# Attention groups 1 and 2 on tokens sorted by residue modulo 4, and the first large transfers requested by SyncE in order

## The chip, the cores and the metric

The kernel runs on one core of one Trainium2 chip. Its engines are TensorE (PE in the rows; PEld is its weight load), VectorE (DVE), ScalarE (ACT), GpSimd (POOL) and SyncE (SP), which here only requests DMA transfers. The metric is the device time of one launch in microseconds, lower being better. Times of a kernel are medians of several launches. The profile is one further launch, and its own time stands beside the others below.

## The reference, cut to what matters

The program is a model of two layers over 256 tokens of width 2048. Each layer normalises x, multiplies it by a wide matrix `w_in`, feeds four mixers (branches A to D) and merges them:

```python
h = _rmsnorm(x, norm_g); proj = h @ w_in            # 2048 x 17544
ya = _branch_dilated(a_q, a_k, a_v, ...) * silu(a_z)  # A: three groups of 4 heads
yb = _branch_mla(...) * silu(b_z); yc = _branch_mlstm(...) * silu(c_z); yd = _branch_s5(...) * silu(d_z)
up = einsum('bsnw,nwd->bsnd', stack([ya, yb, yc, yd]), w_up)
merged = sum(sigmoid(gate + merge_b) * up, over the branches)
return x + merged @ w_out
```

The change is in branch A. Its three groups have windows and dilations `A_GROUPS = ((128, 1), (512, 4), (2048, 16))`: a query of group 1 sees only keys that are a multiple of 4 tokens back, one of group 2 only those a multiple of 16 back. So in both groups a query sees only keys whose token number has the same residue modulo 4. Each head's scores are `q k / sqrt(128) - slope * distance`, masked, and the groups are joined by their log-sum-exp:

```python
o = einsum(p, v) / den;  lse = m + log(den)         # for each group
w = softmax(stack(lses), axis=0);  out = sum(w[..., None] * o_all, axis=0)
```

Inputs, weights and outputs are float32.

## The kernel before

**Weights.** All weights stream through the core. They are cut into units of 128 x 1024 numbers (512 KB; smaller ones for narrow blocks). SP requests a unit into one of four `raw` buffers; ACT rounds it to `wh` and DVE forms the remainder `wl` (four buffers each, `Stream.split`). PE multiplies each unit in three passes: `wh,hH`, `wl,hH` and `wh,hL`, where `hH` and `hL` are the two parts of the normalised, transposed x. A full unit is 12 such matmuls of 128 x 512. `Stream.get(i)` casts three units ahead of PE and requests six ahead. A column block of `w_in` is eight units, and its result lies in two of the four PSUM banks named `mm`.

**Order of the work.** The program is written out by Python code that keeps a plan of the engines' clocks (`Plan`). The weight matmuls are the backbone. After each unit `tick` lets the branches' generators ("chains" a to d, e for evacuations, m, q) emit a step when the plan says that its inputs are ready. Each engine then runs its instructions in the order written, and each waits only by semaphores. A block that needs a branch's result (`until`) forces the chain on.

**Branch A** (`a_evac`, `a_transposes`, `a_group`, `softmax_pv`). For each group the blocks `aq`, `ak`, `av` give queries, keys and values. q and k are transposed on PE (`tt`) and copied by ACT to `aqT` and `akT`. With 256 tokens there are two query tiles of 128. For each of 4 heads the first tile is multiplied with 128 keys, the second with 256 (`sc`). DVE adds the distance term (`as0`, `as1`), ACT takes the exponential, PE transposes three 128 x 128 pieces per head (`pt`), and three matmuls per head multiply them with the values (`pv`). Group 0 is kept in `aO`; the results of groups 1 and 2 are folded in by `rows`. After group 2 `aO` is divided, gated and transposed for the up projection (`y_split`, `yt`).

**The start.** SP requests the parameters `pp`, then parts of the transposed input `xt` and the first units in turn. ACT scales `xt` to `hH` (`prep_first`). ACT also requests the natural input `xb`, four transfers of 512 KB, and the constants `cc` (`first_squares`); the mean square of x is taken from `xb`, and `r`, its inverse root, is first needed when the evacuations of the first block begin. The framework gives each transfer one of eight semaphores in turn, and a request waits until the transfer eight before it has landed.

The instruction wrapper (`call`, line 258) and the `load` helper (line 277) record nearly everything, so the rows go by tile names.

Of the kernel before, what the change touches and what calls it, by code (L numbers as in the profile page):

```python
# [107 lines left out]
for _nm, _n in (("norm_g", 16), ("aqn", 1), ("akn", 1), ("cqg", 4), ("ckvg", 1), ("bqn", 1), ("bkn", 1),  # L108
                ("bqr", 64), ("bkr", 64), ("convw", 16), ("convb", 4), ("ib", 4), ("fb", 4),
                ("lr", 16), ("li", 16), ("ld", 16), ("dskip", 4)):  # L110
    PP[_nm] = (_o, _o + _n)
    _o += _n
# [4 lines left out]
for _nm, _n in (("dist", 768), ("mb", 256), ("mc", 128), ("iota", 256), ("inv", 32)):  # L117
    CC[_nm] = (_o, _o + _n)
    _o += _n
# [144 lines left out]
def hybrid_kernel(ctx: ExitStack, tc: tile.TileContext, x_in, xt_in, pos, win, wup, wout, wuq, wukv, wglu, pp_in, db_in,  # L264
# [22 lines left out]

    cc = const.tile([P, NCC], F32, tag="cc", name="cc")
    ident = const.tile([P, P], F32, tag="ident", name="ident")
    load(nc.scalar, ident, in_=id_in)  # L290
# [69 lines left out]
    class Stream:  # L360
        DL, SL = 6, 3

        def __init__(self):
            self.raw, self.spl, self.names, self.nd, self.ns = {}, {}, {}, 0, 0

        def dma(self, upto, part=None):
            while self.nd <= min(upto, len(units) - 1):
# [9 lines left out]
                self.nd += 1  # L377

# [76 lines left out]
    def block(key, lhs, K, n):  # L455
# [8 lines left out]
        while k < K:  # L464
            assert units[cur[0]][0] == key, (units[cur[0]][0], key)
            lhs(k, 0)
            if cur[0] and not key[0]:
                lhs(min(k + 4, K - 1), 0)
# [85 lines left out]
    def rotary_tables():  # L554
        V.tensor_tensor(sel, ident[:, 0:4], ident[:, 32:36], op=ALU.add)
        G.memset(Mz.bitcast(F32), 0.0)
        pf = const.tile([P, 2], F32, tag="posf", name="posf")
# [37 lines left out]
    def new_layer(l):  # L595
        o = L()
        o.l, o.after = l, []
        o.pp = parp.tile([P, NPP], F32, tag="pp", name="pp")
        load(nc.scalar if l else nc.sync, o.pp, in_=pp_in[l])
        o.p = lambda nm: o.pp[:, PP[nm][0]:PP[nm][1]]  # L600
# [4 lines left out]
        o.r, o.gL, o.yT = None, None, {}  # L605
        return o

    def load_d(o):
        o.db = s4([P, 2, 16, 16], name="db")
        load(nc.sync if o.l else nc.scalar, o.db, in_=db_in[o.l].rearrange("p (r t c) -> p r t c", r=2, t=16))  # L610
        o.dc = s4([P, 2, 16, 32], name="dc")
        load(nc.sync if o.l else nc.scalar, o.dc, in_=dc_in[o.l].rearrange("p (r t c) -> p r t c", r=2, t=16))
# [100 lines left out]
    def to_T(src, dst, scale=None, nh=4):  # L713

        for t in range(2):
            ps = brps("tt").rearrange("p (k s) -> p k s", s=P)
            for k in range(nh):
                T.transpose(ps[:, k], src[:, t, k * P:(k + 1) * P], ident)
            if scale is None:
                A.copy(dst[:, :, t * P:(t + 1) * P], ps[:, :nh])  # L720
            else:
                A.activation(dst[:, :, t * P:(t + 1) * P], ps[:, :nh], AF.Copy, scale=scale)

    def softmax_pv(s0, s1, v, rows):
# [15 lines left out]
        pT = [h2([P, 4, P], name="pT") for _ in range(3)]  # L740
        for i in range(3):
            ps = brps("pt").rearrange("p (k s) -> p k s", s=P)
            for h in range(4):
                src = s0[:, h] if i == 0 else s1[:, h, (i - 1) * P:i * P]
# [3 lines left out]
        for t in range(2):  # L748
            ps = brps("pv").rearrange("p (k s) -> p k s", s=P)
            for h in range(4):  # L750
                for kt in range(t + 1):
                    T.matmul(ps[:, h], lhsT=pT[t + kt][:, h], rhs=v[:, kt, h * P:(h + 1) * P],
                             start=(kt == 0), stop=(kt == t))
# [4 lines left out]
    def a_evac(o, ps, gain_scale, key):  # L758
# [20 lines left out]
        spawn("a", a_transposes(o, dst, key, scale))  # L779

    def a_transposes(o, src, key, scale):
        yield (src,)
        dst = s4([P, 4, S], name=key)
        to_T(src, dst, scale)
        setattr(o, key, dst)

    def a_group(o, g, v):
        qT, kT = o.aqT, o.akT
        yield (qT, kT)
        dist = c_("dist")[:, g * 256:(g + 1) * 256]  # L790
        s0 = h2([P, 4, P], name="as0")
        s1 = s4([P, 4, S], name="as1")
        ps = brps("sc").rearrange("p (k s) -> p k s", s=P)
        for h in range(4):
            T.matmul(ps[:, h], lhsT=qT[:, h, 0:P], rhs=kT[:, h, 0:P], start=True, stop=True)
        for h in range(4):
            V.scalar_tensor_tensor(s0[:, h], dist[:, P:], -SLOPES[4 * g + h], ps[:, h], op0=ALU.mult, op1=ALU.add)
        for h2_ in range(2):
            ps = brps("sc").rearrange("p (k s) -> p k s", s=S)
            for j in range(2):  # L800
                h = 2 * h2_ + j
                T.matmul(ps[:, j], lhsT=qT[:, h, P:], rhs=kT[:, h, :], start=True, stop=True)
            for j in range(2):
                h = 2 * h2_ + j
                V.scalar_tensor_tensor(s1[:, h], dist, -SLOPES[4 * g + h], ps[:, j], op0=ALU.mult, op1=ALU.add)
        yield
        if g == 0:
            o.aO = s4([P, 2, 4, P], name="aO")
            o.amx = parp.tile([P, 2, 4], F32, tag="amx", name="amx")
            o.aden = parp.tile([P, 2, 4], F32, tag="aden", name="aden")  # L810

        def rows(t, ps, mx, den):
            O = o.aO[:, t]
            if g == 0:
                A.copy(O, ps)
                V.tensor_copy(o.amx[:, t], mx[:, t])
                V.tensor_copy(o.aden[:, t], den[:, t])
                return
            al, be, mn = sm([P, 4], name="al"), sm([P, 4], name="be"), sm([P, 4], name="mn")
            V.tensor_tensor(mn, o.amx[:, t], mx[:, t], op=ALU.max)  # L820
            V.tensor_tensor(al, o.amx[:, t], mn, op=ALU.subtract)
            V.tensor_tensor(be, mx[:, t], mn, op=ALU.subtract)
            A.activation(al, al, AF.Exp)
            A.activation(be, be, AF.Exp)
            V.tensor_copy(o.amx[:, t], mn)
            dn = sm([P, 4], name="dn")
            V.tensor_tensor(dn, den[:, t], be, op=ALU.mult)
            V.tensor_tensor(o.aden[:, t], o.aden[:, t], al, op=ALU.mult)
            V.tensor_tensor(o.aden[:, t], o.aden[:, t], dn, op=ALU.add)
            tmp = h2([P, 4, P], name="atmp")  # L830
            for h in range(4):
                A.activation(tmp[:, h], ps[:, h], AF.Copy, scale=be[:, h:h + 1])
                V.scalar_tensor_tensor(O[:, h], O[:, h], al[:, h:h + 1], tmp[:, h], op0=ALU.mult, op1=ALU.add)

        yield from softmax_pv(s0, s1, v, rows)
# [342 lines left out]
    def d_tables(o):  # L1178
# [4 lines left out]
        load_d(o)  # L1183
        yield (o.pp,)
# [215 lines left out]
    xpool = ctx.enter_context(tc.tile_pool(name="xd", bufs=1, space=bass.MemoryType.DRAM))  # L1400
    x_cur = [x_in[:, :, d * 512:(d + 1) * 512] for d in range(4)]

    A.activation(sm([P, 1], name="warm"), one1, AF.Exp)
    o = new_layer(0)
# [7 lines left out]

    first, o.nh = o, 0
    xt = [s4([P, 4, S], name="xt") for _ in range(4)]
    for d in range(4):
        spawn("m", prep_first(o, d, xt[d]))
    load(nc.sync, xt[0][:, 0:1], in_=xt_in[:, 0:1])
# [16 lines left out]
    for l in range(depth):  # L1434
# [35 lines left out]
        for kind, nm in layer_sequence(l):  # L1470
            if kind == "in":
# [49 lines left out]
                elif nm[:2] == "aq":  # L1521
                    spawn("e", a_evac(o, ps, 128.0 ** -0.5, "aqT"))
# [179 lines left out]
```

## Time and profile before

| | us |
|---|---|
| median of 3 runs | 2045.55 (2044.85 to 2045.85) |
| the profiled execution's own time | 2046.62 |
| its span, first to last instruction | 2044.8 |
| PE busy | 2025.2 (99%) |
| DVE busy | 1409.3 (69%) |
| ACT busy | 1037.3 (51%) |
| POOL busy | 170.4 (8%) |
| all DMA traffic | 386.68 MB, mean 189 GB/s |

The span is 1.8 us shorter than the execution's own time, which is 1.1 us above the median. Matmuls overlap in the records (a 128 x 512 one is shown as 390 ns but the next starts 227 ns later), so PE's time is read from stretches and not from the mean of one. Each float32 matmul of branch A (`sc`, `pv`) has two records, a transpose has one.

### The profile page before, as it was taken

Reading aid. Unit: us, or ns where it says so; the run is one execution under the profiler, and the core shown is the slowest. Engines: PE = TensorE matmul, PEld = TensorE weight load, DVE = VectorE, ACT = ScalarE, POOL = GpSimd, SP = SyncE. Lnnn points to the kernel's source line nnn. Section 1 sums busy time; section 2 is a strip of 40 time slices with the busy share of each in tenths; the row PEclk is TensorE's granted clock in tenths of the full one; section 3 lists DMA queues with packets and bytes.
Section 4 is the critical chain, followed back from the end, with each engine's and each line's share of the span. In section 5 each row is a group of like instructions: output and inputs, shape, how many; then the busy total and the mean of one; then the engine's idle time right before and its main releaser. Section 6 shows DMA issues by size and latency. Waiting matters only on the chain.

```text
span 2044.8 us, 26461 instructions
## 1 busy us (share of the span) xinstructions
PE 2025.2 (99%) x9614; PEld 1676.0 (82%) x9614; DVE 1409.3 (69%) x2053; ACT 1037.3 (51%) x1587; POOL 170.4 (8%) x473
## 2 busy tenths in 40 slices
PE   8999999999999999999999999999999999999999
PEld 6788888888878888888887888888888878888887
DVE  5566666698787885656555666758796878756664
ACT  6555446645546444444446555564645454444442
POOL 0331122100110000000032101011001100000000
PEclk9999999999999999999999999999999999999999
DMA  7554555646655566656746544456456546666665
GB/s 288 178 192 165 170 170 160 203 168 191 199 182 170 179 198 207 205 195 210 232 167 209 187 163 166 142 191 194 166 191 197 184 160 192 204 205 202 199 211 172
DMA packets 112898, 386.68 MB, mean 189 GB/s; under 512 B 12544, under 2 KB 15232, under 8 KB 112768
## 3 DMA queue, kind: packets, MB, share of 16 engines
q1 hardware_dynamic: 109088, 377.00, 56.7%
q10 hardware_dynamic: 3680, 8.00, 1.0%
q8 instruction: 75, 1.23, 0.2%
q14 instruction: 55, 0.45, 0.1%
HBM read 380.76 MB, written 4.19 MB: 188 GB/s over the span
## 4 chain that ended last, share of the span: by engine, by line
PE 97%; DMA 1%; ACT 1%; DVE 1%; issue 0%; SPq 0%; ACTq 0%; DVEq 0%
PE mm L258 89%; PE mb L258 2%; DMA raw<-win 1%; PE pv L258 1%; PE tt L258 1%; PE sc L258 1%; ACT wh L258 1%; PE bsc L258 1%; PE pt L258 1%; PE dyp L258 0%; PE dbu L258 0%; PE mt L258 0%; PE cn L258 0%; PE yt L258 0%; PE ckq L258 0%
## 5 line engine op out<-in xcount | busy, mean ns | idle before, releaser
L258 DVE TENSOR_TENSOR wl<-raw,wh 128x1024 fp32r<-128x1024 f32 (+1 forms) x687 | 828.8, 1218 | 513.7 <-ACT wh L258 511.1
L258 ACT CAST wh<-raw 128x1024 fp32r<-128x1024 f32 (+2 forms) x703 | 724.1, 1035 | 778.8 <-PE mm L258 669.9
L258 PE MATMUL mm<-wh,hH 128*128 128x512 f32 (+1 forms) x2240 | 873.4, 393 | 8.3 <-ACT wh L258 5.2
L258 PE MATMUL mm<-wh,hL 128*128 128x512 f32 (+1 forms) x2240 | 863.4, 386 | 0.0
L258 PE MATMUL mm<-wl,hH 128*128 128x512 f32 x2176 | 849.6, 390 | 2.4 <-DVE wl L258 2.4
L258 PEld LDWEIGHTS mm<-wh,hH 128*128 128x128 f32 x2240 | 421.6, 188 | 97.6 <-ACT wh L258 6.7
L258 PEld LDWEIGHTS mm<-wh,hL 128*128 128x128 f32 x2240 | 421.8, 188 | 86.0
L258 PEld LDWEIGHTS mm<-wl,hH 128*128 128x128 f32 x2176 | 409.9, 188 | 86.5 <-DVE wl L258 3.8
L258 PE MATMUL mm<-wh,yH 128*128 128x512 f32 x256 | 100.9, 394 | 3.1 <-ACT wh L258 1.2
L258 PE MATMUL mm<-wh,mH 128*128 128x512 f32 x256 | 100.2, 392 | 0.0
L258 PE MATMUL mm<-wh,yL 128*128 128x512 f32 x256 | 99.7, 390 | 0.0
L258 PE MATMUL mm<-wl,yH 128*128 128x512 f32 x256 | 99.7, 389 | 0.0
L258 PE MATMUL mm<-wh,mL 128*128 128x512 f32 x256 | 99.7, 389 | 0.0
L258 PE MATMUL mm<-wl,mH 128*128 128x512 f32 x256 | 99.6, 389 | 0.0
L258 PEld LDWEIGHTS mm<-wh,yH 128*128 128x128 f32 x256 | 48.1, 188 | 15.2 <-issue 2.4
L258 POOL TENSOR_SCALAR ass<-ass 128x8 f32<-128x8 f32 x12 | 2.6, 214 | 680.1 <-ACT aqk L258 680.1
L258 PEld LDWEIGHTS mm<-wh,yL 128*128 128x128 f32 x256 | 48.1, 188 | 10.1
L258 PEld LDWEIGHTS mm<-wh,mL 128*128 128x128 f32 x256 | 48.1, 188 | 9.9
L258 PEld LDWEIGHTS mm<-wl,mH 128*128 128x128 f32 x256 | 48.1, 188 | 9.8
L258 PEld LDWEIGHTS mm<-wh,mH 128*128 128x128 f32 x256 | 48.1, 188 | 9.8
L258 PEld LDWEIGHTS mm<-wl,yH 128*128 128x128 f32 x256 | 48.1, 188 | 9.5
L258 DVE TENSOR_TENSOR dm<-dm,dm 128x256 f32<-128x256 f32 x128 | 48.6, 421 | 1.6
(364 smaller groups left out, 1529.1 us busy)
## 6 DMA issues: line engine op xcount, KB each, us to landing
raw<-win SPq DMA_DIRECT2D x543, 512.0 KB, 4.2
raw<-wup SPq DMA_DIRECT2D x64, 512.0 KB, 4.2
raw<-wout SPq DMA_DIRECT2D x64, 512.0 KB, 4.2
mb<-mb_in SPq DMA_DIRECT2D x32, 256.0 KB, 4.6
raw<-wuq SPq DMA_DIRECT2D x6, 512.0 KB, 4.5
raw<-win SPq DMA_DIRECT2D x16, 136.0 KB, 2.1
xb<-x_in ACTq DMA_DIRECT2D x4, 512.0 KB, 10.8
raw<-wglu SPq DMA_DIRECT2D x4, 512.0 KB, 4.4
```

The costliest lines, as they stand in the source:

```text
L258: return fn(*args, **kw)
```

## The change

Four things are edited.

1. In groups 1 and 2 the tokens stand sorted by their residue modulo 4: 64 tokens of residue 0, 64 of residue 1 (tile 0), then 2 and 3 (tile 1). A query of tile 0 then has no key in tile 1. q and k are sorted for free of extra instructions by ACT's copy out of PSUM (`to_T(..., sorted_=True)`). Scores become two 128 x 128 pieces per head, transposes and value products two per head (`diag`). The distance table for these groups is one 128 x 128 tile in which other residues are masked.
2. Values lie with tokens on partitions, so they are sorted by a round trip through DRAM (`through`): SP writes `av` out in one transfer and reads it back as two halves of 64 partitions. Group 1's result and its maxima and sums are no longer folded into group 0's at once. They are kept sorted (`aO[1]`, `ast[1]`); group 2 is folded into them, and then they go through DRAM back to the natural order and are joined with group 0. That makes three round trips in a layer, six in all. Between write and read-back the generator lets 3.5 us of the plan's PE clock pass.
3. At the start ACT requests only the small `ng` (the norm gains, taken out of `pp`), `ident` and `pos`. `pp`, the four `xb`, `cc`, `db` and `dc` are requested by SP, one each behind units 4 to 9 (`Stream.extra`).
4. In the first layer units are requested four ahead up to unit 4, and `hH` is prepared one step earlier (`k + 5`).

```diff
         def dma(self, upto, part=None):
...
                 self.nd += 1
+                for f in self.extra.pop(self.nd - 1, ()):
+                    f()
...
-            self.dma(i + self.DL)
+            self.dma(i + (self.DL if i > 4 else 4))
...
     def first_squares(o):
-        xb = [s4([P, 2, 512], name="xb") for _ in range(4)]
-        yield
         for d in range(4):
-            load(nc.scalar, xb[d], in_=x_cur[d])
-            plan.ready[xb[d].name] = (plan.ready[xb[d].name][0] + 6000.0, "DMA")
-        load(nc.scalar, cc, in_=cc_in)
-        for d in range(4):
-            yield from squares(o, d, xb[d])
+            yield (lambda: d in xf,)
+            if d not in xf:
+                stream.dma(4 + d)
+            yield from squares(o, d, xf[d])
...
             for k in range(nh):
                 T.transpose(ps[:, k], src[:, t, k * P:(k + 1) * P], ident)
+            out, in_ = dst[:, :, t * P:(t + 1) * P], ps[:, :nh]
+            if sorted_:
+                out = dst.rearrange("p h (r m) -> p h r m", r=4)[:, :, :, 32 * t:32 * t + 32]
+                in_ = in_.rearrange("p h (m r) -> p h r m", r=4)
...
+    def through(tile, n, sort):
+
+        d = xpool.tile([S, n], F32, tag=f"perm{n}", name=f"perm{n}")
+        nat = d.rearrange("(t p) c -> p t c", t=2)
+        srt = d.rearrange("(m t r) c -> r m t c", t=2, r=2)
+        halves = [(tile[64 * r:64 * r + 64], srt[r]) for r in range(2)]
+        whole = [(tile, nat)]
+        for a, b in whole if sort else halves:
+            nc.sync.dma_start(out=b, in_=a)
+        at = plan.clk["PE"] + 3500.0
+        yield (lambda: plan.clk["PE"] > at,)
+        for a, b in halves if sort else whole:
+            nc.sync.dma_start(out=a, in_=b)
+        plan.ready[tile.name] = (plan.clk["PE"] + 5000.0, "DMA")
+
     def a_group(o, g, v):
         qT, kT = o.aqT, o.akT
-        yield (qT, kT)
...
+        yield (qT, kT, v)
+        if g:
+            yield from through(v, 512, True)
+            yield (qT, kT)
         s0 = h2([P, 4, P], name="as0")
...
+        if g:
+            s1 = h2([P, 4, P], name="as1")
+            dist = c_("dist")[:, S + (g - 1) * P:S + g * P]
+            for t, s in ((0, s0), (1, s1)):
+                ps = brps("sc").rearrange("p (k s) -> p k s", s=P)
+                q = slice(t * P, (t + 1) * P)
+                for h in range(4):
+                    T.matmul(ps[:, h], lhsT=qT[:, h, q], rhs=kT[:, h, q], start=True, stop=True)
...
+        yield from softmax_pv(s0, s1, v, rows, diag=g > 0)
+        if g == 2:
+            one, st1 = o.aO[1].rearrange("p t h d -> p t (h d)"), o.ast[1].rearrange("p t a h -> p t (a h)")
+            both = [through(one, 512, False), through(st1, 8, False)]
...
+            yield (one, st1)
+            for t in range(2):
...
+                join(o.aO[0], o.ast[0], t, st1[:, 0], st1[:, 1], other)
...
+    stream.extra = {4: [lambda: load(nc.sync, o.pp, in_=pp_in[0])], 8: [lambda: load(nc.sync, cc, in_=cc_in)],
+                    9: [lambda: load_d(o)]}
+    for d in range(4):
+        stream.extra.setdefault(4 + d, []).append(lambda d=d: first_x(d))
```

**Order, place 1: ACT and SP at the start.** ACT before, from its first full unit on (`raw` is a weight unit, `wh` its rounded half, `xt` the transposed input, `hH` its scaled first part, `DMAHW` a semaphore of a transfer):

```order
11 L258 CAST wh<-raw 128x1024 [waits DMAHW0_49]
12 L277 DMA xb<-x_in 128x2x512 x2
13 L277 DMA xb<-x_in 128x2x512 [waits DMAHW2_49]
14 L277 DMA xb<-x_in 128x2x512 [waits DMAHW3_49]
15 L277 DMA cc<-cc_in 128x1440 [waits DMAHW4_49]
16 L258 ACTIVATE hH<-xt,pp 128x256 [waits DMAHW1_49]
17 L258 ACTIVATE hH<-xt,pp 128x256 x3
```

ACT after, the same place:

```order
12 L258 CAST wh<-raw 128x1024 [waits DMAHW0_49]
13 L258 ACTIVATE hH<-xt,ng 128x256 [waits DMAHW1_49]
14 L258 ACTIVATE hH<-xt,ng 128x256 x3
15 L258 CAST wh<-raw 128x1024 [waits DMAHW2_49]
16 L258 ACTIVATE hH<-xt,ng 128x256 [waits DMAHW3_49]
17 L258 ACTIVATE hH<-xt,ng 128x256
18 L258 CAST wh<-raw 128x1024 [waits DMAHW4_49]
19 L258 CAST wh<-raw 128x1024 [waits DMAHW6_49,DVE_49]
```

The five requests have left ACT, and with them three waits for earlier transfers that stood ahead of the scaling of the second quarter of `xt`. They stand on SP now, each behind a unit:

```order
12 L277 DMA raw<-win 128x1024 [waits DMAHW6_49,DVE_49]
13 L277 DMA pp<-pp_in 128x217 [waits DMAHW7_49]
14 L277 DMA xb<-x_in 128x2x512 [waits DMAHW0_49]
15 L277 DMA raw<-win 128x1024 [waits DMAHW1_49,DVE_49]
16 L277 DMA xb<-x_in 128x2x512 [waits DMAHW2_49]
17 L277 DMA raw<-win 128x1024 [waits DMAHW3_49,DVE_49]
18 L277 DMA xb<-x_in 128x2x512 [waits DMAHW4_49]
19 L277 DMA raw<-win 128x1024 [waits DMAHW5_49,DVE_49]
```

**Place 2: PE, group 1 of the first layer.** Before (scores, transposes of the probabilities, value products; weight matmuls between them left out):

```order
1803 L258 MATMUL sc<-akT,aqT 128x128 x4
1804 L258 MATMUL sc<-akT,aqT 128x256 x4
...
1853 L258 MATMUL pt<-ident,as_4037 128x128 x4
1854 L258 MATMUL pt<-ident,as_4038 128x128 x8
...
1867 L258 MATMUL pv<-av,pT 128x128 x12
```

After:

```order
1826 L258 MATMUL sc<-akT,aqT 128x128 x8
...
1887 L258 MATMUL pt<-ident,as_4086 128x128 x4
1888 L258 MATMUL pt<-ident,as_4087 128x128 x4
...
1913 L258 MATMUL pv<-av,pT 128x128 x8
```

Four score matmuls are half as wide, and four transposes and four value products are gone; the same holds for group 2 and for the second layer.

**Place 3: SP around group 2 of the first layer.** Before, between two requests for `mb` there are only weight units:

```order
48 L277 DMA mb<-mb_in 128x512
49 L277 DMA raw<-win 128x1024 x2
50 L277 DMA raw<-wup 128x1024 x2
51 L277 DMA raw<-win 128x1024 x14
52 L277 DMA mb<-mb_in 128x512
```

After (`perm` is the DRAM buffer, `av` the values, `aO` and `ast` the result of groups 1 and 2 with its maxima and sums):

```order
67 L807 DMA perm_5783<-av 128x2x512
68 L277 DMA raw<-win 128x1024
69 L811 DMA av<-perm_5783 64x2x512 x2
70 L277 DMA raw<-wup 128x1024 x2
71 L277 DMA raw<-win 128x1024 x9
72 L807 DMA perm_6155<-aO 128x1x512 x2
73 L807 DMA perm_6158<-ast 128x1x8 x2
74 L277 DMA raw<-win 128x1024 x2
75 L811 DMA aO<-perm_6155 128x2x512
76 L811 DMA ast<-perm_6158 128x2x8
77 L277 DMA raw<-win 128x1024 x3
```

Two round trips have come in, with one and two weight units between a write and its read-back, which must wait on SP for the write.

## Rows read from the trace of the kernel before

**Rows 1.** The page: busy time of the engines, and two costliest groups.

```profile
span 2044.8 us, 26461 instructions
...
PE 2025.2 (99%) x9614; PEld 1676.0 (82%) x9614; DVE 1409.3 (69%) x2053; ACT 1037.3 (51%) x1587; POOL 170.4 (8%) x473
...
L258 DVE TENSOR_TENSOR wl<-raw,wh 128x1024 fp32r<-128x1024 f32 (+1 forms) x687 | 828.8, 1218 | 513.7 <-ACT wh L258 511.1
L258 ACT CAST wh<-raw 128x1024 fp32r<-128x1024 f32 (+2 forms) x703 | 724.1, 1035 | 778.8 <-PE mm L258 669.9
```

**Rows 2.** Chain of waits, first layer, groups 1 and 2: start, us, what.

```profile
435.52 0.91 PE sc L258 x8
...
641.18 2.62 PE sc L258 x16
643.80 2.73 PE mm L258 x12
...
655.97 1.31 PE pt L258 x12
...
660.04 2.68 PE pv L258 x24
```

**Rows 3.** Timeline of PE, 14 to 20 us: start, us, instruction, idle before.

```profile
18.34 0.50 PE L258 MATMUL mm<-wh,hH 128*128 128x512 f32 x1 [3.50 <-ACT wh L258]
19.60 0.80 PE L258 MATMUL mm<-wl,hH 128*128 128x512 f32 x1 [0.76 <-DVE wl L258]
```

**Rows 4.** Timeline of ACT and of its requests, 9 to 17 us.

```profile
9.26 4.67 ACTq L277 DMA_DIRECT2D xb<-x_in  x4
15.25 0.35 ACTq L277 DMA_DIRECT2D cc<-cc_in  x1
15.65 1.70 ACT L258 ACTIVATE hH<-xt,pp 128x256 fp32r<-128x256 f32 x4 [5.34 <-DMA raw<-win]
```

**Rows 5.** Windows: us, busy of PE, PEld, DVE, ACT, POOL; PEclk, DMA share, GB/s.

```profile
0.00:8.00 8.00, 5.18 (x12) 1.78 (x13) 1.85 (x7) 3.60 (x7) 0.20 (x4) 1.00 0.71 217
8.00:16.00 8.00, 6.84 (x23) 5.12 (x22) 2.70 (x5) 2.30 (x4) 0.00 (x0) 0.79 1.01 402
...
9.10:12.40 3.30, 3.30 (x9) 2.61 (x8) 1.60 (x2) 1.04 (x1) 0.00 (x0) 0.51 1.01 402
...
19.60:22.70 3.10, 3.10 (x8) 2.48 (x9) 3.10 (x5) 3.10 (x6) 0.00 (x0) 0.52 1.06 395
```

**Rows 6.** Timeline of SP's requests, 0 to 5 us.

```profile
0.74 0.39 SPq L277 DMA_DIRECT2D pp<-pp_in  x1
1.18 0.42 SPq L277 DMA_DIRECT2D xt<-xt_in  x1
...
4.49 0.44 SPq L277 DMA_DIRECT2D raw<-win  x1
```

**Rows 7.** That unit's transfer (window 4.4 to 4.8 us): KB, us to landing.

```profile
raw<-win SPq DMA_DIRECT2D x1, 512.0 KB, 7.6
```

**Rows 8.** Timelines of ACT and PE near 60 us.

```profile
59.92 1.16 ACT L258 ACTIVATE blat<-mm,bss 128x448 f32<-128x448 f32 x2 [3.06 <-DVE bss L258]
...
60.61 0.39 PE L258 MATMUL mm<-wh,hH 128*128 128x272 f32 x1 [1.48 <-ACT blat L258]
```

**Rows 9.** DMA issues, whole run: count, KB each, median us to landing.

```profile
raw<-win SPq DMA_DIRECT2D x543, 512.0 KB, 4.2
...
xd<-xb ACTq DMA_DIRECT2D x4, 512.0 KB, 5.1
xb<-xd SPq DMA_DIRECT2D x4, 512.0 KB, 6.1
```

**Rows 10.** Waits of SP, whole run: us in total, times, longest.

```profile
SPq L277 <- DVE wl L258: 1525.2, 623, 10.2
```

More of the change, by code (lines that the diff above doesn't have):

```diff
@@ L605, in new_layer @@
         o.r, o.gL, o.yT = None, None, {}
+        o.aO, o.ast = {}, {}
         return o
@@ L711, in copy_r, with to_T @@
         return dst
-    def to_T(src, dst, scale=None, nh=4):
+    def to_T(src, dst, scale=None, nh=4, sorted_=False):
         for t in range(2):
@@ L750, in softmax_pv, with a_evac @@
             for h in range(4):
-                for kt in range(t + 1):
-                    T.matmul(ps[:, h], lhsT=pT[t + kt][:, h], rhs=v[:, kt, h * P:(h + 1) * P],
-                             start=(kt == 0), stop=(kt == t))
+                for i, kt in ((t, t),) if diag else ((t + kt, kt) for kt in range(t + 1)):
+                    T.matmul(ps[:, h], lhsT=pT[i][:, h], rhs=v[:, kt, h * P:(h + 1) * P],
+                             start=(diag or kt == 0), stop=(kt == t))
             rows(t, ps, mx, den)
         yield
-    def a_evac(o, ps, gain_scale, key):
+    def a_evac(o, ps, gain_scale, key, g):
         dst = s4([P, 2, 512], name="aqk")
@@ L796, in a_group @@
[L796 to L805, printed above, removed]
@@ L835, in a_group, with rows, other @@
-        yield from softmax_pv(s0, s1, v, rows)
+            V.tensor_tensor(dn, den, be, op=ALU.mult)
+            V.tensor_tensor(st[:, t, 1], st[:, t, 1], al, op=ALU.mult)
+            V.tensor_tensor(st[:, t, 1], st[:, t, 1], dn, op=ALU.add)
+            for h in range(4):
+                V.scalar_tensor_tensor(O[:, t, h], O[:, t, h], al[:, h:h + 1], other(h, be[:, h:h + 1]),
+                                       op0=ALU.mult, op1=ALU.add)
+        def rows(t, ps, mx, den):
+            O, st = o.aO[i], o.ast[i]
+            if g < 2:
+                A.copy(O[:, t], ps)
+                V.tensor_copy(st[:, t, 0], mx[:, t])
+                V.tensor_copy(st[:, t, 1], den[:, t])
+                return
+            tmp = h2([P, 4, P], name="atmp")
+            def other(h, be):
+                A.activation(tmp[:, h], ps[:, h], AF.Copy, scale=be)
+                return tmp[:, h]
+            join(O, st, t, mx[:, t], den[:, t], other)
@@ new lines, in a_group, with other @@
+        yield from softmax_pv(s0, s1, v, rows, diag=g > 0)
+        if g == 2:
+            one, st1 = o.aO[1].rearrange("p t h d -> p t (h d)"), o.ast[1].rearrange("p t a h -> p t (a h)")
+            both = [through(one, 512, False), through(st1, 8, False)]
+            for part in both:
+                next(part)
+            at = plan.clk["PE"] + 3500.0
+            yield (lambda: plan.clk["PE"] > at,)
+            for part in both:
+                for _ in part:
+                    pass
+            yield (one, st1)
+            for t in range(2):
+                O1, st1 = o.aO[1][:, t], o.ast[1][:, t]
+                def other(h, be):
+                    A.activation(O1[:, h], O1[:, h], AF.Copy, scale=be)
+                    return O1[:, h]
+                join(o.aO[0], o.ast[0], t, st1[:, 0], st1[:, 1], other)
+                yield
+            o.aO, o.aden = o.aO[0], o.ast[0][:, :, 1]
```

126 lines of the change are left out of this document (71 added, 55 removed).

## The prediction

> **What bounds the kernel now.** I read the page's busy times first [rows 1]: PE is busy for 2025.2 of 2044.8 us, DVE for 69% and ACT for 51%. So 19.6 us is all that PE ever waits, and the rest of the time is PE's own instructions. Two questions are left: how much PE work goes, and what happens to the 19.6 us.
>
> For the first I read the chain of waits around branch A [rows 2]: the scores of a group are one piece of 2.62 us, its transposes 1.31, its value products 2.68, with weight matmuls on either side and no idle between. They stand in line with the weights, so what they lose the span loses.
>
> For the second I read PE's timeline at the start [rows 3]. The first quarter of `xt` is used up at about 14.8 us; then PE idles 3.50 and, one matmul later, 0.76 us. ACT's timeline says why [rows 4]: from 9.26 to 15.6 us its queue stands in five requests, and the scaling of the second quarter of `xt` is queued behind them. The row blames a weight transfer; the reader should see that a request that waits for a semaphore blocks an engine as an instruction does. After that idle the granted clock is 0.52 from 19.6 to 22.7 us, the 1.2 GHz level [rows 5].
>
> **The change part by part.**
>
> *Scores.* Four matmuls of 128 columns take 0.91 us [rows 2], 0.2275 each, so the four of 256 columns take 2.62 - 0.91 = 1.71, 0.4275 each. Eight of 128 columns are 1.82: 0.80 us less. *Transposes*: 1.31 / 12 = 0.109; four fewer, 0.44. *Value products*: 2.68 / 12 = 0.223; four fewer, 0.89. Together 2.13 us a group, and with two groups in two layers **8.5 us**. PE gets nothing new: sorting q and k rides on copies that ACT makes anyway, and sorting the values is DMA. Those ACT copies now read PSUM at a stride, which no row shows: between their price now and twice that, on an engine that is busy half the time and mostly waits for PE's buffers (the 669.9 us behind its casts [rows 1]), so I take nothing.
>
> *Round trips.* Six, each 512 KB out and back, 6.3 MB beside 387: nothing for bandwidth. A write took 5.1 us and a read of what was written 6.1 [rows 9]; these are whole-partition transfers, and sorted ones are not in the trace. What is queued behind the read-back on SP is the next weight unit, and for that ACT's cast, DVE's remainder and PE wait. How late may it be? A buffer `raw` is free when the remainder is done, 1.04 + 1.22 us after its cast begins [rows 1]; the next unit lands 4.2 us later [rows 9], at 6.5 us. The same buffer is cast again after four units, 4 x 2.73 = 10.9 us [rows 2], so it lies ready for 4.4 us. Its cast runs three units, 8.2 us, ahead of PE and needs 2.3, another 5.9. SP can so be 10.3 us late once before PE sees it. That it lives with this room now is in its waits: 1525 us behind the freeing of buffers [rows 10]. A whole trip of 11.2 us, less the 2.7 us or more of the weight unit between write and read-back, keeps SP at most 8.5 us. I take 0, the nearest reading; the bounds are 0 and, without any of the time between, 0.9 us for each trip, 5.4 in all. The values are wanted by PE only after scores and softmax, 16 us after the scores' end in group 2 [rows 2], so PE doesn't wait for the trip itself. A join that finds its data late holds ACT, whose casts have the same 5.9 us.
>
> The Trainium skill speaks against these trips: "SBUF — State Buffer", section "Door 1: The DMA port swizzle", says that 64 partitions of one half reach 8 of the 16 DMA ports, and "Can I just issue two DMAs to hit both halves?" there says that two such transfers at once gain little. No transfer here shows it. By its 196 GB/s against 328 the sorted side of a trip would take, as an estimate, 2.7 us for 512 KB where it took 1.6; a trip stays within the room above, and the sum doesn't move.
>
> *First matmul.* SP's first request is `pp`, and the next starts 0.44 us later [rows 6]. Without it all others come 0.44 us sooner, and 0.12 MB less is ahead of them: **0.45 us**, with 0.3 and 0.9 as bounds.
>
> *The idle after the first quarter.* Without the requests ACT can scale the second quarter when it has landed, before 12.1 us: the unit requested after it at 4.49 lands 7.6 us later [rows 6, 7]. Its cast and remainder, 2.26 us, are then done at about 14.4, when PE gets there (14.84 less the 0.45). Both waits go, **4.26 us**, and with them the second fall of the clock: 3.1 us at 0.52 [rows 5] lose 3.1 x 0.48 = **1.5 us**. The first fall, 9.1 to 12.4 at 0.51, comes before the change bites and stays.
>
> *What is late next.* PE then runs about 6 us earlier against transfers that come no faster than 402 GB/s [rows 5]. Take unit 5 (counted from 0). With it and ahead of it go `xt` 2.1 MB, six units 3.15, `pp`, `ident`, `ng` 0.18 and one `xb` 0.52: 5.95 MB. By 8 us 217 x 8 = 1.74 MB have moved; the rest needs 10.5 us, so 18.5, less 0.45. Transfers overlap: the unit of [rows 7] had 2.75 MB with and ahead of it, due at 10.5, and landed at 12.1. With 1.6 to 2.3 us for that, unit 5 lands at 19.6 to 20.3. The squares of the first `xb`, a pair of scalings, cast and remainder take 4.4 us on ACT and DVE: 22.4 to 23.4 with what overlaps. PE wants it three units after unit 2, at 14.84 - 0.45 + 3 x 2.73 = 22.6. So unit 5, and unit 6 likewise, may be late by 0 to 0.7 us each; from unit 7 on there is over 1 us of room. I take **1.2 us** of new idle; bounds 0, and 4.3, which is all that was won.
>
> *The narrow block at 60 us.* PE waits 1.48 us there [rows 8]: ACT's `blat`, which frees the PSUM bank, stands behind DVE's `bss`, 3.06 us late. In the new order `bss` is done ahead of the narrow units' remainders, so the wait goes: **1.5 us**. Bounds 0 and 1.5.
>
> *The rest.* DVE and ACT lose some elements and gain one join; neither sets the end. Every step of the later order shifts a little, and the 19.6 - 4.26 - 1.48 = 13.9 us of PE's other idle can be reshuffled; I take no change, bounds -3 and +7 (half as much again).
>
> **Sum** against the profiled execution: -8.5 - 0.45 - 4.26 - 1.5 + 1.2 - 1.5 = -15.0, so 2046.6 - 15.0 = 2031.6. That execution is 1.1 us above the median of the runs, hence **2030.5**.
>
> **Rivals.**
>
> *A. The transfers set the start.* The 4.26 us and the fall of the clock come back behind units 5 to 10, since all of `xb`, `cc`, `db`, `dc` must still come through in 35 us. For it: 392 to 402 GB/s without a break up to the twenties [rows 5]. Against it: in the new order units stand ahead of these loads, and the byte count leaves units 2 to 4 on time. -8.5 - 0.45 - 1.5 = -10.4: 2035.1.
>
> *B. New waits in the later order.* The planner shifts nearly every step of branches A and D, and a longer-held `as1` shares its pool with branch D. For it: those 13.9 us show that the order has such waits. Against it: DVE has 31% free. +7 on the sum: 2037.5.
>
> *C. The trips starve the weights: slower than before.* Place: the read-back on SP, with the next unit behind it. If small rows (`ast` goes out in pieces of 32 bytes) or half-partition transfers make a trip hold SP for more than 10.3 us, PE pays the rest six times. The kernel is slower from 10.3 + 15 / 6 = 12.8 us on. At twice the 11.2 us it would pay 12.1 x 6 = 72 us: 2103. Against it: it needs over half as much again as any two such transfers took [rows 9]; and `ast` is 16 KB in all.
>
> "DMA: Bandwidth & Descriptors", section "Specifications", in the Trainium skill, asks for 512 bytes or more in a piece for full rate; by that rule only `ast` would suffer, and no run here shows it.
>
> **Chances.** Forecast 0.70, A 0.14, B 0.12, C 0.04. The forecast's own range is 2026 to 2034: with no new idle and the first clock fall also gone it is 15 + 1.2 + 1.6 = 17.8 us, 2027.7, and a luckier order takes a little more. A and B reach to 2038. Low 2025, high 2039 leaves out C and some of B. What a measurement of this kernel can tell from no change is about 0.2%, 4.1 us: faster means below 2041.5. The forecast, A and B are all below it but for a B that is twice its price. Faster 0.93, same 0.04, slower 0.03.
>
> **What would show it.** Right: PE's first two waits after 14 us together under 1.5 us, granted clock 1.00 from 13 us on, scores of groups 1 and 2 in 1.8 us with 16 records, value products in 1.8 with 16; no PE wait behind casts near the round trips; PE's busy time about 10 us less, idle about 5 less. Wrong: PE idle that ends with ACT's `wh` shortly after a read-back (C); a series of waits for `wh` between 20 and 40 us (A); busy time down by 10 but idle up (B).

## The result, and the profile after

| | before | after |
|---|---|---|
| median of the runs, us | 2045.7 (2044.85 to 2049.46, 4 runs) | 2034.68 (2032.78 to 2036.13, 4 runs) |
| span of the profiled execution, us | 2044.8 | 2031.0 |
| PE busy, us | 2025.2 | 2014.3 |

The ratio is 0.994, 95% interval 0.9927 to 0.9952: 0.6% faster, within the predicted range, 4 us above the predicted time. A second set of five launches beside nine of before gave 2034.03 and 0.9941 (0.9929 to 0.9954). Launches of one kernel differ by several us, and the profiled one of the changed kernel is the fastest of its four: from profile to profile the time fell from 2046.62 to 2032.78, by 13.8 of the 15.0 us forecast, so part of the 4 us is the spread of launches.

The page of the changed kernel, its first lines, against [rows 1]:

```profile
span 2031.0 us, 26412 instructions
...
PE 2014.3 (99%) x9566; PEld 1665.8 (82%) x9566; DVE 1405.7 (69%) x2061; ACT 1036.2 (51%) x1587; POOL 173.2 (9%) x473
```

PE's busy time is 10.9 us less and its idle (span less busy) went from 19.6 to 16.7. PE has 48 records fewer: in each of four groups 4 transposes with one and 4 value products with two.

The chain of waits of the changed kernel around group 2 of the first layer (start, us, what), against [rows 2]:

```profile
644.46 1.78 PE sc L258 x16
646.24 10.90 PE mm L258 x48
657.14 0.87 PE pt L258 x8
658.01 2.73 PE mm L258 x12
660.75 1.78 PE pv L258 x16
```

Scores, transposes and value products take 4.43 us where they took 6.61. The same three durations stand at groups 1 and 2 of the second layer. That is 2.18 us a group, 8.7 in all four. ACT's copies that sort q and k cost no more than before: the median is 590 ns for `akT` in both kernels, and 682 where it was 685 for `aqT`.

PE's timeline at the start, against [rows 3] (start, us, instruction, idle before it):

```profile
8.38 0.50 PE L258 MATMUL mm<-wl,hH 128*128 128x512 f32 x1 [0.22 <-DVE wl L258]
10.53 0.50 PE L258 MATMUL mm<-wh,hH 128*128 128x512 f32 x1 [0.73 <-ACT wh L258]
11.78 0.50 PE L258 MATMUL mm<-wl,hH 128*128 128x512 f32 x1 [0.76 <-DVE wl L258]
```

The 4.26 us of idle are gone and 1.49 us stand at another place. Stretches of the start as in [rows 5] (length, PE busy and its matmuls, granted clock, DMA share, GB/s):

```profile
8.00:16.00 8.00, 6.29 (x25) 1.00 1.02 414
9.10:12.40 3.30, 1.81 (x8) 1.00 1.03 420
19.60:22.70 3.10, 3.10 (x15) 1.00 1.03 395
```

In this launch the granted clock stays at 1.00, the 2.4 GHz level, where before it was 0.51 and 0.52. It doesn't in every launch: in a second profile of the same kernel (experiment 4), after an idle of 0.98 and 0.77 us at 10.5 and 11.8 us, it is 0.68 from 13 to 18 us:

```profile
13.00:18.00 5.00, 5.00 (x17) 0.68 1.04 402
```

So far all goes the predicted way. But the first 128 x 272 matmul of the narrow block, at 60.61 us before [rows 8], starts at 56.06 with no wait, and the store of the first layer's output begins at 955.69 where it began at 960.74: 4.6 us ahead early, 5.0 at the layer's end. Groups 1 and 2 of that layer should have added 4.4 to this, and before's idle ahead of them some more. Gains are eaten at two new places. The first is PE near 41 us:

```profile
41.28 0.51 PE L258 MATMUL mm<-wh,hH 128*128 128x512 f32 x1 [1.46 <-ACT wh L258]
42.54 0.51 PE L258 MATMUL mm<-wl,hH 128*128 128x512 f32 x1 [0.76 <-DVE wl L258]
```

and ACT's timeline there:

```profile
39.11 0.31 ACT L258 ACTIVATE bj<-mm,r 128x64 f32<-128x64 f32 x1 [3.80 <-DVE r L258]
...
40.17 2.94 ACT L258 CAST wh<-raw 128x1024 fp32r<-128x1024 f32 x3
```

`bj`, the first step of branch B that reads `r`, now stands in ACT's order directly behind the making of `r`. It waits 3.8 us, and three casts that PE needs stand behind it. (Before, `r` was done at 44.9 us and `bj` began at 49.2, behind casts; now `r` is done at 39.0, 5.9 us earlier, but `bj` is placed 10 us earlier.) The second place is PE at 600 to 630 us:

```profile
602.28 0.47 PE L258 MATMUL mm<-wh,yH 128*128 128x512 f32 x1 [0.38 <-DVE aqk L258]
609.83 0.47 PE L258 MATMUL mm<-wh,hH 128*128 128x512 f32 x1 [0.94 <-DVE gate L258]
620.23 0.50 PE L258 MATMUL mm<-wh,hH 128*128 128x512 f32 x1 [1.94 <-ACT wh L258]
621.49 0.79 PE L258 MATMUL mm<-wl,hH 128*128 128x512 f32 x1 [0.76 <-DVE wl L258]
```

where before had one wait, of 1.21 us:

```profile
610.10 0.47 PE L258 MATMUL mm<-wh,yH 128*128 128x512 f32 x1 [1.21 <-ACT wh L258]
```

ACT in the changed kernel, and then the two steps of DVE that matter:

```profile
617.22 1.07 ACT L258 COPY akT<-tt 128x512 f32<-128x512 f32 x2 [5.72 <-DVE gate L258]
618.18 1.07 ACT L258 ACTIVATE dk<-dr 128x1024 f32<-128x1024 f32 x1
619.14 3.88 ACT L258 CAST wh<-raw 128x1024 fp32r<-128x1024 f32 x4
```

```profile
608.93 1.41 DVE L258 SCALAR_TENSOR_TENSOR gate<-mm,r,mb 128x512 f32<-128x512 f32 x2 [5.02 <-PE tt L258]
...
615.96 1.22 DVE L258 TENSOR_TENSOR gate<-gate 128x1024 f32<-128x1024 f32 x1
```

`akT` is a copy of a transpose out of PSUM; nothing in it needs `gate`. It waits for DVE's addition on `gate` because its buffer comes from the pool `s4`, whose 31 buffers are all in use: the results of groups 1 and 2 (`aO[1]`) and the sorted values now live there longer. In the order of before the same copy waits for PE alone:

```profile
616.72 1.08 ACT L258 COPY akT<-tt 128x512 f32<-128x512 f32 x2 [1.59 <-PE tt L258]
```

Four casts stand behind `akT`, and PE pays 1.94 and 0.76 us for it. The 0.94 us come from the same pool one step earlier: DVE's first step on a new `gate`, also from `s4`, waits 5.02 us for PE's transposes, and the addition at 615.96 us is late by that (experiment 2 takes both waits away). With the 0.38 us behind `aqk`, PE idles 4.0 us in this stretch. The granted clock then falls to 0.83 for 10 us.

The round trips, by SP's waits (us in total, times, longest), against [rows 10]:

```profile
SPq L277 <- DVE wl L258: 1468.1, 607, 9.5
...
SPq L811 <- DMA perm<-av: 9.5, 4, 3.9
...
SPq L811 <- DMA perm<-aO: 2.0, 2, 1.4
```

and their landings (issues, size, median us to landing), against [rows 9]:

```profile
perm<-av SPq DMA_DIRECT2D x4, 512.0 KB, 6.2
av<-perm SPq DMA_DIRECT2D x8, 256.0 KB, 4.8
...
aO<-perm SPq DMA_DIRECT2D x2, 512.0 KB, 4.7
perm<-ast SPq DMA_DIRECT2D x4, 4.0 KB, 4.4
```

No read-back keeps SP for more than 3.9 us, and no wait of PE stands near one.

### The profile page after: what moved, and what is told of

It reads as the page before. It is cut to its first block, busy times and chain, and to the rows that moved or that the text cites. A ratio compares the mean times of both kernels' runs of the same rounds, so it can differ in the third digit from the quotient of the medians.

```text
span 2031.0 us, 26412 instructions
## 1 busy us (share of the span) xinstructions
PE 2014.3 (99%) x9566; PEld 1665.8 (82%) x9566; DVE 1405.7 (69%) x2061; ACT 1036.2 (51%) x1587; POOL 173.2 (9%) x473
## 4 chain that ended last, share of the span: by engine, by line
PE 69%; ACT 0%; DVE 0%; issue 0%; DMA 0%; ACTq 0%
PE mm L258 64%; PE mb L258 1%; PE pv L258 1%; PE tt L258 0%; PE sc L258 0%; PE mt L258 0%; ACT wh L258 0%; PE dyp L258 0%; PE pt L258 0%; PE bsc L258 0%; PE dbu L258 0%; DMA raw<-win 0%; PE yt L258 0%; PE xt L258 0%; PE cn L258 0%
## 5 line engine op out<-in xcount | busy, mean ns | idle before, releaser
L258 PEld LDWEIGHTS mm<-wh,yH 128*128 128x128 f32 x256 | 48.1, 188 | 12.6 <-issue 2.7
L258 DVE SCALAR_TENSOR_TENSOR gate<-mm,r,mb 128x512 f32<-128x512 f32 x64 | 44.9, 743 | 8.9 <-PE tt L258 5.0
```

Of the source, the lines that this page charges most:

```text
L258: return fn(*args, **kw)
```

## The experiments

Theory: attention gives its 8.7 us, the start some 5, the trips cost nothing, and two new waits, each an instruction at the head of ACT's queue with casts behind it, take back part. Rivals: the trips cost time; the start's gain is lost later; the stall at 600 us is not the pool.

**1. The two halves of the change, each alone.** `start_only` has the edits 3 and 4 on the kernel before, `attn_only` the edits 1 and 2.

```diff
 # start_only: the start of after, branch A of before
+            self.dma(i + (self.DL if i > 4 else 4))
+                lhs(min(k + 5, K - 1), 0)
+    stream.extra = {4: [...pp], 8: [...cc], 9: [lambda: load_d(o)]}
 # attn_only: branch A of after, the start of before
+        if g:
+            yield from through(v, 512, True)
+        yield from softmax_pv(s0, s1, v, rows, diag=g > 0)
```

Expected of `start_only`:

> Only the new start on the kernel before; attention as it was. Theory: the first 128x272 matmul of the narrow block comes 4.5 us earlier (60.6 to about 56.1), with new PE waits of about 2.2 us near 41 us, and nothing takes this back later: about 2041.0 us, 0.998 of before. Rival: the later order takes it back in waits (the planner shifts steps): 2044 to 2046, with the narrow block early and the output not. A second rival: without the attention edits the start gives more, since the waits of before at 1070 to 1090 us (2.2 us and a clock of 0.83) go too: about 2038.

Expected of `attn_only`:

> Only the sorted attention on the kernel before; the start as it was, with both its PE waits (3.5 and 0.76 us after 18 us) and its fall of the clock. Theory: attention gives 8.7 us (2.2 a group, four groups) and the copy akT of group 2 in the first layer, which waits for a free slot of the s4 pool, gives back about 4.4 us between 600 and 630 us: 2041.3 us, 0.998 of before. Rival: the wait at 600 to 630 us belongs to the order that only both parts together make; then attention alone gives all of its 8.7 us, 2037 us, 0.9957.

Measured: `start_only` 2043.38 us (2041.05 to 2046.36, 11 runs) beside 2046.83 of before, ratio 0.9984 (0.9975 to 0.9993). `attn_only` 2038.46 (2037.0 to 2039.11, 5 runs), ratio 0.9959 (0.9947 to 0.9972). The halves, 3.4 and 8.4 us by medians, add up to 11.8, near the whole change's 11.0 and 12.6. For `start_only` neither holds: 2.4 us above the theory's 2041.0 and under the rival's 2044 to 2046, with launches from 2041 to 2046; the second rival's 2038 falls, the waits at 1070 to 1090 us (2.8 us) stand. For `attn_only` both theories were half right: the stall at 600 to 630 us is there (4.0 us of idle), so it belongs to the attention edits alone; but the time is that of the rival, since the new order lacks waits that before had (0.5 us near 690 and 1.47 at 1670 to 1690 among them). In `start_only` the PE wait near 41 us is there, larger (3.45 us between 30 and 50 us), and the clock fell behind it. These are its stretch and the same stretch of the changed kernel:

```profile
44.00:50.00 6.00, 5.61 (x17) 0.72 0.49 155
```

```profile
44.00:50.00 6.00, 6.00 (x28) 1.00 0.51 156
```

**2. One more buffer.** The order of the instructions is the same on every engine; `akT` loses its wait for DVE.

```diff
-S4B, H2B, WARM = 31, 9, 10
+S4B, H2B, WARM = 32, 9, 10
```

> The changed kernel with 32 instead of 31 buffers in the s4 pool, all instructions in the same order. Theory: the copy akT of group 2 in the first layer no longer waits for DVE's gate addition; the idle of PE at 620 us (1.94 and 0.76) and the fall of the clock after it (0.83 for 10 us) go: 3 to 4.4 us, about 2030.5 us, 0.998 of the changed kernel. Rival: akT is late for its place in the order and the casts behind it wait for something else: the time stays within 1 us of the changed kernel, and an idle of 2 to 3 us stays between 600 and 630 us.

Measured: 2028.79 us (2026.97 to 2030.74, 4 runs), ratio to before 0.9913 (0.99 to 0.9927) where the changed kernel has 0.994. Between 600 and 630 us PE idles 0.38 instead of 4.0 us and the clock stays up:

```profile
600.00:610.00 10.00, 9.62 (x47) 1.00 0.56 171
610.00:620.00 10.00, 10.00 (x46) 1.00 0.56 184
620.00:630.00 10.00, 10.00 (x56) 1.00 0.55 187
```

In the changed kernel the same three stretches are

```profile
600.00:610.00 10.00, 8.68 (x42) 1.00 0.31 102
610.00:620.00 10.00, 8.29 (x36) 1.00 0.33 105
620.00:630.00 10.00, 9.01 (x32) 0.83 0.60 195
```

Both kernels stand within 0.1 us of each other at 602 us, and the scores of group 2 then start at 638.24 instead of 644.30: 6.0 us, of which 3.6 are idle and about 1.7 clock (10 us at 0.83); the other 0.7 were not traced. The medians, of two sets of launches, differ by 5.9 us, the ratios by 5.5. ACT's timeline in this kernel shows `akT` waiting for its transpose and for nothing else:

```profile
608.79 1.08 ACT L258 COPY akT<-tt 128x512 f32<-128x512 f32 x2 [1.58 <-PE tt L258]
```

The cause is the pool; the rival falls. The expectation was too low because the 0.94 us ahead of the stall went too: DVE's first step on `gate` no longer waits. The 0.38 us behind `aqk` stay.

**3. No trips.** This kernel leaves the sorting of values and results out; the order on PE, ACT and DVE is unchanged.

```diff
-        for a, b in whole if sort else halves:
-            nc.sync.dma_start(out=b, in_=a)
...
-        for a, b in halves if sort else whole:
-            nc.sync.dma_start(out=a, in_=b)
```

> The changed kernel without the 24 transfers of the six round trips through DRAM: values and group results stay in the order they have, so the sorting of values and outputs is left out of what is computed; all engines but SP have the same instructions in the same order. Theory: the trips cost nothing, the time is within 1 us of the changed kernel, and the idle at 600 to 630 us stays, since it is a pool's slot. Rival: each trip costs PE up to 0.9 us (behind late weights), or delays the chain of group 2: 2 to 5.4 us less than the changed kernel, and idle behind ACT's casts gone near the trips.

Measured: 2036.05 us (2033.59 to 2038.31, 5 runs), ratio 0.9949 (0.9936 to 0.9961): no faster than the changed kernel, whose interval overlaps. The stall is the same, so it is not made by a late trip:

```profile
622.83 0.50 PE L258 MATMUL mm<-wh,hH 128*128 128x512 f32 x1 [1.99 <-ACT wh L258]
624.09 0.50 PE L258 MATMUL mm<-wl,hH 128*128 128x512 f32 x1 [0.76 <-DVE wl L258]
```

**4. The changed kernel again**, with no edit. Expected:

> The changed kernel itself, in more launches, to size what varies by launch and to share its runs of before with the three others. Theory: the idle near 41 us and at 600 to 630 us stands in every launch, and the granted clock falls after it in some launches only, so the times spread over 3 to 5 us with the lower clock in the longer ones: about 2035 us, 0.994 of before. Rival: the spread comes from the transfers at the start: then the idle before 30 us differs, and the clock doesn't.

Measured: 2034.03 us (2032.12 to 2036.63, 5 runs). The mean granted clock is 0.999 in the launches of 2032.12 and 2032.68 us, and 0.997 in those of 2034.03, 2036.51 and 2036.63, as expected. In its profile the clock between 620 and 630 us is 0.66 where the first profile had 0.83, and between 13 and 18 us 0.68 where that had 1.00, with the same instructions and much the same idle (near 41 us 1.38 instead of 2.22). The idle before 30 us differs little (1.75 against 1.49 us at 10.5 and 11.8), and the clock does differ, so the rival falls as far as two profiles can tell.

**5. One more buffer, again.** Expected:

> The changed kernel with 32 buffers in the s4 pool once more, beside the changed kernel and beside the next run. Theory: 5.3 us less than the changed kernel (3.6 of idle between 600 and 630 us, 1.7 of the clock behind it): about 2029.5 us. Rival: the first look was a favoured set of launches, and 3 us or less remain.

Measured: 2028.68 us (2028.49 to 2029.12, 4 runs), 0.9914 (0.99 to 0.9927); 5.35 us less than the changed kernel in the same set. The theory holds.

**6. The step that reads `r` later.** With the 32 buffers:

```diff
+        plan.ready[r.name] = (plan.ready[r.name][0] + 3000.0, "DVE")
         yield (r,)
...
-                    if o.r is None:
+                    if o.r is None or not l:
                         continue
```

In the first layer the head of branch B is now left to the chain of `r`, which the plan believes 3 us later.

> 32 buffers in the s4 pool, and in the first layer the step of branch B that reads r (the head of bj, kr and then blat) stands five casts later on ACT, so that ACT no longer waits 3.8 us for r with three casts behind it. Theory: the PE idle of 2.0 to 2.5 us near 41 us goes, and with it the fall of the clock that follows it in some launches (1.7 to 3.4 us where it was seen): 2.2 to 4 us less than with 32 buffers alone, about 2026 us, and a smaller spread. Rival: the step is now late for what needs it, and PE waits at the narrow block at 56 to 60 us for blat, as the kernel before did (1.5 us): 2028 to 2029 us.

Measured: 2026.39 us (2025.89 to 2027.51, 4 runs), ratio to before **0.9903** (0.9889 to 0.9916), 2.3 us less than with the buffer alone and with no launch in common. This version beats both kernels. PE doesn't wait between 38 and 50 us:

```profile
38.00:44.00 6.00, 6.00 (x27) 1.00 0.57 191
44.00:50.00 6.00, 6.00 (x28) 1.00 0.32 92
```

and the narrow block has no wait for `blat`: the rival falls.

**7. Every trip made twice.** The second pass sorts what is sorted already, so values and results stand in another order than they should.

```diff
         for a, b in whole if sort else halves:
             nc.sync.dma_start(out=b, in_=a)
+        for a, b in halves if sort else whole:
+            nc.sync.dma_start(out=a, in_=b)
+        for a, b in whole if sort else halves:
+            nc.sync.dma_start(out=b, in_=a)
```

> The changed kernel with each round trip made twice, out, back, out, back, on SP: the second write has to wait for the first read-back, so SP stands for 11 us at a time for the values and near 19 us at the group's result, against 2.4 us on the mean in the changed kernel. If SP has 10.3 us of room once, as reckoned, PE pays about 1.2 us at the first late unit and 3.7 in all for each of four trips of the values, and about 9 us for each of the two results: some 33 us, with falls of the clock up to 45: 2068 to 2080 us, and idle behind ACT's wh at each trip. If the room is far larger (the theory that trips are free at any plausible length), less than 5 us. If SP has no room at all, 4 x 14 + 2 x 19 us: 2130 us.

Measured: 2065.66 us (2063.75 to 2068.27, 5 runs), ratio to before 1.0093 (1.0079 to 1.0107); 31.6 us more than the changed kernel, just under the 33 to 45 reckoned. SP at the first trip (start, us, what):

```profile
432.17 0.43 SPq L807 DMA_DIRECT2D perm<-av  x1
439.16 1.19 SPq L809 DMA_DIRECT2D av<-perm  x2
443.90 0.37 SPq L811 DMA_DIRECT2D perm<-av  x1
444.37 0.42 SPq L277 DMA_DIRECT2D raw<-wup  x1
```

From 432.2 to 443.9, 11.7 us, no weight is requested, and PE pays for it some 8 us later:

```profile
451.73 0.50 PE L258 MATMUL mm<-wl,yH 128*128 128x512 f32 x1 [0.74 <-DVE wl L258]
456.52 0.47 PE L258 MATMUL mm<-wh,hH 128*128 128x512 f32 x1 [1.08 <-ACT wh L258]
```

1.8 us for 11.7, where a room of 10.3 us leaves 1.4. At the two results, where SP requests no weight for 17.0 us (684.2 to 701.2) and 18.5 (1706.3 to 1724.8), PE idles 5.7 us (700 to 710) and 8.6 (1720 to 1740); 10.3 us of room leaves 6.7 and 8.2. The room that the prediction worked out is about right. But the second result is no clean case of it: there ACT stands in the join, with the casts behind it, since DVE waits for the result's maxima and sums to be read back:

```profile
1730.10 0.16 DVE L258 TENSOR_TENSOR mn<-ast 128x4 f32<-128x4 f32 x1 [13.72 <-DMA ast<-perm]
```

The other three trips of the values cost 1.15, 1.36 and 1.50 us, at attention's own steps. All six together are 20 us of idle; PE's busy time is 11.3 us longer at a mean granted clock of 0.993. So the 33 us reckoned for idle alone were too many, 3.7 for each trip of the values above all. Rival C's mechanism is real; the change stays on the free side of it.

**8. The start alone without its new wait.** `start_only` with the edit of experiment 6 (31 buffers).

> The kernel before with the new start alone, and the step of branch B that reads r five casts later, so that the wait near 41 us should be gone. Theory: the start is worth what the prediction's terms for it say once this wait is taken out: 0.45 + 4.26 + 1.5 - 1.2 + 1.5 = 6.5 us, with the first fall of the clock (1.6 us) not surely gone, so 2039 to 2041 where before is 2046.7; ratio 0.997. Rival: the start alone is worth no more than the 3.4 us measured with the wait, since what it wins is waited for elsewhere: 2043.

Measured: 2041.53 us (2040.56 to 2043.52, 7 runs) beside 2047.05, ratio 0.9975 (0.9963 to 0.9986): 5.1 us by the ratio, 2.8 to 7.6 by its interval, and a spread of 3 us instead of 5. The theory's 2039 to 2041 is just missed; the rival's 2043 is not excluded by the interval, but only one of seven launches reaches it. The wait for `r` is gone, but PE still idles 0.51 and 0.73 us at 37.7 and 41.5 us, the latter behind a cast that waited 1.28 us for its weight unit.

**9. Sorted attention once more, one launch.** Despite its label, `attn32` is the kernel of `attn_only`, with 31 buffers.

> Sorted attention on the kernel before, the start as it was: another look at the start for its clock, and at 600 to 630 us. Theory: idle of 4.0 us at 600 to 630 us again; the fall of the clock at 9 us, which the kernel before showed with the same instructions at the start, is there in one launch and not in another.

Measured: 2037.65 us; idle of 4.1 us at 600 to 630 us again, this time at a clock of 1.00. At the start the clock has no fall at 9 us:

```profile
9.00:10.00 1.00, 1.00 (x4) 1.00 1.01 414
...
18.00:20.00 2.00, 1.33 (x2) 0.50 1.04 405
20.00:22.00 2.00, 2.00 (x6) 0.50 1.04 389
```

The fall behind the idle of 16 to 20 us is there in all four profiles of kernels with the old start (before, this one, `attn_only` and the next); the fall at 9 us in that of before alone.

**10. Sorted attention with 32 buffers**, the old start.

```diff
-S4B, H2B, WARM = 31, 9, 10      # in attn_only
+S4B, H2B, WARM = 32, 9, 10
```

> Sorted attention on the kernel before, the start as it was, and 32 buffers in the s4 pool. Theory: the idle of 4.0 us at 600 to 630 us and the fall of the clock behind it (1.7 us) go, so 5 us or more less than with 31 buffers (2038.5 then): about 2033 where before is 2046.7, ratio 0.9935. That is more than the 8.7 us of PE work, by the waits of before that the new order lacks (0.7 at 600, 0.5 at 690, 1.5 at 1680 us, and the clock at 1080). Rival: without the new start the stall has another cause (ACT behind, not the slot): 2037 to 2038.5.

Measured: 2032.81 us (2031.36 to 2033.55, 5 runs), ratio 0.9933 (0.9919 to 0.9947). 14.1 us by medians beside 2046.94 (10.8 to 16.6 by the interval), more than the changed kernel's 11.0 and 12.6, without any of the new start. PE idles 0.38 us between 600 and 630, so the rival falls.

## Why the prediction was right, and where it wasn't

- **Attention's PE work** (8.5): right. 8.7 measured, by the same three pieces of the chain. The sorted copies on ACT, put at nothing without a row, cost nothing more.
- **First matmul earlier** (0.45, bounds 0.3 and 0.9): mis-sized. It starts at 7.01 us in before and 6.70 to 7.32 in the four profiles with the old start; with the new one at 5.04 to 5.42 in eight profiles of nine (6.32 in `notrips`): about 1.7 us. Most of it is waited for again at 10.5 and 11.8 us.
- **Idle after the first quarter** (4.26) **and the second fall of the clock** (1.5): right, both gone. The new start alone does it: no PE idle between 12.5 and 20 us in any profile that has it. That the five requests in ACT's queue were the cause rests on [rows 4]; they were not moved apart from the rest of the new start. A fall of the clock at 13 to 18 us can come all the same, behind the new idle at 10.5 and 11.8 us (0.68 in `after_again`, 0.81 in `head_later`).
- **The first fall of the clock stays**: wrong as put. Of four profiles with the old start only that of before has it (experiment 9). About 1.7 us of the difference between the two profiles are this.
- **New idle at units 5 and 6** (1.2): wrong place. In the changed kernel's profile no wait over 0.1 us stands between 12.5 and 30 us. Idle came at 10.5 to 12.5 us (1.49, against the earlier first matmul) and near 41 us (2.22), the latter no transfer but `r`.
- **Narrow block** (1.5): right, no wait for `blat` in the changed kernel. In `attn_only`, with the old start, the 1.48 us stand there still. The new start as a whole, with the early reader of `r` out of the way, is worth 5.1 us (experiment 8) or 6.4 (experiment 6 against 10, by medians); the prediction's terms for it sum to 6.5.
- **Round trips** (0): right. Without them nothing is won (experiment 3), and at double length PE pays about what the room of 10.3 us leaves over (experiment 7). SP's longest wait behind a read-back was 3.9 us, where up to 8.5 were reckoned. By "SBUF — State Buffer", section "Door 1: The DMA port swizzle", of the Trainium skill a transfer on 64 partitions reaches half of the ports, which made 1.1 us in the prediction's estimate. The landings can't tell: a whole transfer of 512 KB took 3.1 to 6.9 us, the halves of 256 KB 4.0 to 6.4 (medians of a pair). By "Specifications" in "DMA: Bandwidth & Descriptors" of the Trainium skill pieces under 512 bytes fall short of full rate, here only those of `ast`. The trace has 4 KB of them in 4.4 us, near what 512 KB took, and nothing waited for them.
- **The rest** (0, bounds -3 and +7): here lies most of the miss. It was the sum of three terms that cancel in part. The new order of branch A lacks waits of before: 5.4 us (experiment 10: 14.1 less 8.7, with 2.1 to 7.9 by the interval). The two profiles show 3.7 of it as idle that is gone: 0.8 at 600 to 620 us, 0.5 at 690 to 710, 0.9 at 1070 to 1090 and 1.5 at 1660 to 1700. The full pool costs 5.4 to 5.9 (experiments 2 and 5); the early reader of `r` 2.3 (experiment 6). Net +2.3 to +2.8, more than half of the 4 us by which the prediction was low. That the net came out small is luck: the prediction had none of the three.

Of the signs that the prediction named for being right, PE's records and durations and its busy time (10.9 us less) came true. The first two waits after 14 us make 2.22 us instead of under 1.5, and the idle fell by 2.9 us instead of 5, both for the two new waits; the clock was at 1.00 from 13 us on in the first profile only, and there up to 620 us.

Of the rivals, A is refuted for the changed kernel: with transfers at 395 to 414 GB/s from 8 to 30 us there is no series of waits for `wh`. In the two kernels with the start alone PE has single waits of 0.3 to 0.7 us for `wl` between 34 and 42 us, and there casts do wait for their weight unit (3.5 us at 32.6 us in `start_only`). B was right in kind and not in place: the pool that runs out is not the one that took `as1` but `s4`. The price was near: it named 7, and the two new waits together take 7.7 to 8.2. Its time, 2037.5, was missed because the gain of the new order stands against it. C did not occur. The forecast and B were set against each other with chances of their own, but they were not alternatives: both happened.

What stays open: why the new order lacks each of the waits of before was not tried one by one; which of the longer-lived tiles fills the pool; and what makes the clock fall in one launch and not in the next after much the same idle.

## What to carry to other kernels

When a buffer's life gets longer, list every tile of its pool and ask who is next to need a slot: the wait shows up in an instruction that has nothing to do with the change, and costs what is queued behind it. Look at each queue's head after a reorder, not only at the queue that was relieved: moving requests off ACT let `r` come earlier, and with it an early reader that blocked three casts. A transfer that holds a request queue costs PE nothing up to the slack of the buffers behind it; here that slack, worked out from the trace, held to about 1 us when the transfers were doubled.

## What the runs showed of the hardware

- With the same instructions the granted clock differs from launch to launch. After the idle near 41 us it stayed at 1.00 in the first profile of the changed kernel, and was 0.65 from 44 to 50 us in that of `notrips`, which has the same instructions on PE. After the 4 us at 600 to 630 us it was 0.83, 0.66 and, in `attn32`, 1.00. In `after_again` it was 0.68 from 13 to 18 us, where the first profile had 1.00. So an idle of 2.2 us near 41 us cost nothing more in one launch, and one of 2.5 us cost some 2.1 us more in `notrips` (0.65 over 6 us). This fits the spreads in part only: 4.5 us in five launches of the changed kernel, 1.6 in four where both new waits are gone, but also 0.6 and 3.8 in the two sets with one of them left.
- In the changed kernel 4 KB out in 32-byte pieces took 4.4 us, and 8 KB back the same, near the 4.7 to 6.2 of 512 KB (medians).
